# Fourier feature products of a diffusion backbone: from 4-byte operand pairs to 16-bit pairs with a power-of-two scale

## The chip, the cores and the metric

The kernel runs on one core of a Trainium2 chip. The metric is the device time of one execution in microseconds, taken as the median of several runs. The core's engines each work through a queue of their own in order: TensorE (PE, its weight loads PEld), VectorE (DVE), ScalarE (ACT), GpSimd (POOL), and SyncE (SP), which issues the transfers.

## The reference

Two layers work on 2048 latent tokens and 256 context tokens of width 1024. One input projection feeds three groups of heads: 2-D Fourier mixing, chunked spatial gating, and attention with 8 heads. Each result is gated, the three are joined, and one output projection with a gated residual ends the layer. The part that matters here is the Fourier group:

```python
def _fourier(u):
    b, n, _ = u.shape
    ug = u.astype(jnp.float32).reshape(b, n, F_GROUPS, F_GROUP_DIM).transpose(0, 2, 1, 3)
    f = jnp.fft.fft2(ug, norm="ortho").real
    return f.transpose(0, 2, 1, 3).reshape(b, n, F_WIDTH).astype(u.dtype)
...
    f_out = (_fourier(f_in) @ w_fmix) * jax.nn.silu(f_gate)
```

F_WIDTH is 256. The transform along the 64 features of a group is folded into the input projection and into `w_fmix`; the transform along the tokens is done in the kernel.

## The kernel before, in words

**Precision.** Nearly every product works on pairs: a value is split into a high and a low half, and `mm3` issues three matmuls into one accumulator, high x high, high x low, low x high. Almost everywhere the halves are 16-bit floats (F16). The last step of the Fourier group and the output projection still use 4-byte halves (F32R).

**The order.** The whole program is first recorded as a list of operations in program order (`Plan`). Then `schedule` lays them out by a list scheduler with a price for each operation (`cost`), planned ends of transfers, buffer counts and a look-ahead, and issues them; each engine's order is pinned to what came out. The three matmuls of an `mm3` are one operation (`plan.group`). The price of a matmul by the kind of its moving operand:

```python
        elif rhs.dtype == F16:
            d = n / 2.4 + 3.4 if args[1].shape[0] > 64 else n / 4.8 + 75.0
        else:
            d = max(190.0, n / 2.4 + 15.0)
```

with n the columns, and 20 more for a group of F16 matmuls.

**Stages.** In a layer, blocks of token tiles are normed and projected (`block`), with matmuls into `pj`. Then comes `attention`: for 8 heads, blocks of four query tiles run over 18 key tiles in pairs. A pair takes six matmuls for the scores (`sc`), two exponentials per key tile on ScalarE (`pp`, and `pw` or `sc` in place), one subtraction per key tile for the low half, on GpSimd for three of four and on VectorE for the fourth (`pp`), and, a few pairs later, 18 matmuls with the values (`pv`). Ahead of them run the maxima of the scores: matmuls into two banks of `mx`, and a VectorE reduction of each, with a small transposed shift at the end of a block (`mneg`, `mh`, `m`, `h`). After attention comes the output projection (`mixed`, `outward`).

**The background.** Work that attention does not need is fed in between the pairs by a generator, `background`: from the tenth pair on, two turns per pair. Its first part is `fourier`, where each `yield` stands for 6 turns in layer 0 and 8 in layer 1; then follow the modulation vectors of the gate and, in layer 0, the preparation of the next layer's weights, which includes several calls of `power`.

**`fourier`.** It loads the mixing weights of the layer (`wfm`, 128 x 4 x 256), adds and subtracts pairs of them (`first`) and splits the three results into `fm` with `split` (a ScalarE copy for the high half, a subtraction on GpSimd for the low one). It loads the 16 projected tiles into `X` and forms a butterfly over them on VectorE. For each of 9 frequency classes (and 2 of the context in layer 0) `finish` makes F16 halves `V`, multiplies them with trigonometric tables `ct`, splits the result `o` into `st0` and `st1`, and multiplies these with `fm`. Classes 1 to 7 are used twice: a mirrored copy `sr` of the halves serves the mirrored frequencies. That makes 18 such products in layer 0 and 16 in layer 1, each of two `mm3`. The result is multiplied with the column `back`, which undoes the scales, and with the gate `fg`, and is stored.

**`power`.** It turns a column of maxima into a scale: a transpose on TensorE, a VectorE maximum of one row, four one-element VectorE operations that give a power of two and its inverse, a TensorE product with a row of ones that spreads both over the partitions, and a VectorE copy.

Of the kernel before, what the change touches and what calls it, by code (L numbers as in the profile page):

```python
# [10 lines left out]
F32 = mybir.dt.float32  # L11
F32R = mybir.dt.float32r
F16 = mybir.dt.float16
# [8 lines left out]
P = 128  # L22
# [41 lines left out]

GK, GQ, G1, G2, G3 = 416, 512, 512, 256, 512
TOP = 14
PTOP, CTOP = 29, 14
KTOP = 11
EXPO = 0x7F800000

# [479 lines left out]
def hybrid_kernel(ctx: ExitStack, tc: tile.TileContext, a: dict, out: bass.AP):  # L550
# [3 lines left out]
    def mk(p, shape, dt, tag, bufs=None):  # L554
        return plan.tile(p, shape, dt, tag, bufs or p.bufs)
# [25 lines left out]
    def f(ap):  # L581
        return ap.bitcast(F32)
# [106 lines left out]
    def split(hi, lo, x, leng=None):  # L689
        act.activation(out=hi, in_=x, func=AF.Copy)  # L690
        (leng or dve).tensor_tensor(out=lo, in0=x, in1=f(hi), op=ALU.subtract)
# [578 lines left out]
    CA, CB = math.cos(math.pi / 8), math.sin(math.pi / 8)  # L1270

    def fourier(l, y, pf):
        back = mk(pf, [P, 1], F32, "back", 1)
        dve.tensor_scalar(out=back, in0=y["ic"][1], scalar1=2.0 ** (PTOP - CTOP), scalar2=None, op0=ALU.mult)
        fm = mk(pf, [P, 6, 256], F32R, "fm", 1)
        wfm = mk(pf, [P, 4, 256], F32, "wfm", 1)
        sp.dma_start(out=wfm, in_=a["w_fmix"][l].rearrange("k p n -> p k n"))
        first = wfm[:, 0]
        flip = column(C_FLIP)
        for s in range(3):  # L1280
            w, z = wfm[:, 2 * (s > 0)], wfm[:, 2 * (s > 0) + 1]
            if s == 2:
                dve.tensor_scalar(out=w, in0=w, scalar1=flip, scalar2=None, op0=ALU.mult)
            dve.tensor_tensor(out=first, in0=w, in1=z, op=ALU.subtract if s == 1 else ALU.add)
            split(fm[:, 2 * s], fm[:, 2 * s + 1], first, pool)
            yield

        def finish(re, im, cs, views):

            ct = mk(pf, [P, 4, P], F16, "ct")  # L1290
            sp.dma_start(out=ct, in_=cs)
            V = [mk(pf, [P, 2, 256], F16, f"V{q}") for q in range(2)]
            n = P + 4
            parts = [(0, re, slice(0, n), 1.0), (1, re, slice(n, 256), -1.0)]
            if im is not None:
                parts += [(0, im, slice(n, 256), 1.0), (1, im, slice(0, n), 1.0)]
            for v, x, s, sg in parts:
                act.activation(out=V[0][:, v, s], in_=x[:, s], func=AF.Copy, scale=sg)
                dve.scalar_tensor_tensor(out=V[1][:, v, s], in0=x[:, s], scalar=sg, in1=V[0][:, v, s], op0=ALU.mult, op1=ALU.subtract)
            if im is None:  # L1300
                for q in range(2):
                    dve.tensor_scalar(out=V[q][:, 0, n:], in0=re[:, n:], scalar1=0.0, scalar2=None, op0=ALU.mult)
                    dve.tensor_scalar(out=V[q][:, 1, P:n], in0=re[:, P:n], scalar1=0.0, scalar2=None, op0=ALU.mult)
            o = bank([P, 2, P])
            for g in range(2):
                gs_ = slice(g * P, (g + 1) * P)
                two = g == 1 or im is not None
                mm3(o[:, g], V[0][:, 0, gs_], V[1][:, 0, gs_], ct[:, 0], ct[:, 1], True, not two)
                if two:
                    mm3(o[:, g], V[0][:, 1, gs_], V[1][:, 1, gs_], ct[:, 2], ct[:, 3], False, True)  # L1310
            sh_ = [mk(pf, [P, 2, P], F32R, f"st{q}") for q in range(2)]
            split(sh_[0], sh_[1], o)
            for gate_rows, out_rows, w in views:
                if w == 4:
                    sr_ = [mk(pf, [P, 2, P], F32R, f"sr{q}", 1) for q in range(2)]
                    for s, r in zip(sh_, sr_):
                        dve.tensor_copy(out=r, in_=f(s)[:, :, ::-1])
                    sh_ = sr_
                fg = mk(pf, [P, 256], F32, "fg")
                sp.dma_start(out=fg, in_=gate_rows)  # L1320
                o = bank([P, 256])
                mm3(o, sh_[0][:, 0], sh_[1][:, 0], fm[:, 0], fm[:, 1], True, False)
                mm3(o, sh_[0][:, 1], sh_[1][:, 1], fm[:, w], fm[:, w + 1], False, True)
                dve.scalar_tensor_tensor(out=fg, in0=o, scalar=back, in1=fg, op0=ALU.mult, op1=ALU.mult)
                sp.dma_start(out=out_rows, in_=fg)

        X = mk(pf, [P, NCK, 256], F32, "X", 1)
        W = mk(pf, [P, 8, 256], F32, "W", 1)
        Q = mk(pf, [P, 8, 256], F32, "Q", 1)
        if l < DEPTH - 1:  # L1330
            for t in range(CT):
                sp.dma_start(out=Q[:, t], in_=p_d[t])
            pool.tensor_tensor(out=Q[:, 2], in0=Q[:, 0], in1=Q[:, 1], op=ALU.add)
            pool.tensor_tensor(out=Q[:, 3], in0=Q[:, 0], in1=Q[:, 1], op=ALU.subtract)
            gv, mv = (v.rearrange("(t k) f -> k t f", k=CT) for v in (fgc_d, mfc_d))
            for k in range(CT):
                finish(Q[:, 2 + k], None, a["cs_c"][k], [(gv[k], mv[k], 2)])
                yield
        for t in range(NCK):
            sp.dma_start(out=X[:, t], in_=p_d[CT + t])  # L1340

        def tt_(o, i0, i1, op):
            dve.tensor_tensor(out=o, in0=i0, in1=i1, op=op)

        def ts_(o, i0, k):
            dve.tensor_scalar(out=o, in0=i0, scalar1=k, scalar2=None, op0=ALU.mult)

        def lin(o, i0, k0, i1, k1):
            ts_(o, i0, k0)
            dve.scalar_tensor_tensor(out=o, in0=i1, scalar=k1, in1=o, op0=ALU.mult, op1=ALU.add)  # L1350

        A_, S_ = ALU.add, ALU.subtract
        x = lambda i, n=1: X[:, i:i + n]
        w = lambda i, n=1: W[:, i:i + n]
        q = lambda i, n=1: Q[:, i:i + n]
        gv, mv = (v.rearrange("(t k) f -> k t f", k=NCK) for v in (fgx_d, mfx_d))

        def both_ways(k):
            r = [(gv[k], mv[k], 2)]
            if 0 < k < NCK // 2:  # L1360
                r.append((gv[NCK - k], mv[NCK - k], 4))
            return r

        def fin(k, re, im):
            finish(re[:, 0], None if im is None else im[:, 0], a["cs_x"][k], both_ways(k))

        tt_(w(0, 8), x(0, 8), x(8, 8), A_)
        yield
        tt_(x(8, 8), x(0, 8), x(8, 8), S_)
        yield  # L1370
        tt_(x(0, 4), w(0, 4), w(4, 4), A_)
        yield
        tt_(x(4, 4), w(0, 4), w(4, 4), S_)
        yield
        tt_(w(0, 2), x(0, 2), x(2, 2), A_)
        yield
        tt_(w(2, 2), x(0, 2), x(2, 2), S_)
        yield
        tt_(x(0), w(0), w(1), A_)
        yield  # L1380
        tt_(x(1), w(0), w(1), S_)
        yield
        fin(0, x(0), None)
        yield
        fin(8, x(1), None)
        yield
        fin(4, w(2), w(3))
        yield
        tt_(w(6), x(5), x(7), S_)
        tt_(w(7), x(5), x(7), A_)  # L1390
        yield
        ts_(w(6, 2), w(6, 2), R2)
        tt_(x(2), x(4), w(6), A_)
        tt_(x(3), x(4), w(6), S_)
        yield
        tt_(w(4), x(6), w(7), A_)
        tt_(w(5), w(7), x(6), S_)
        fin(2, x(2), w(4))
        yield
        fin(6, x(3), w(5))  # L1400
        yield
        rev = X[:, 15:12:-1]
        tt_(q(0, 3), x(9, 3), rev, S_)
        yield
        tt_(q(3, 3), x(9, 3), rev, A_)
        ts_(x(4), q(1), R2)
        ts_(x(5), q(4), R2)
        yield
        tt_(x(6), x(8), x(4), A_)
        tt_(x(7), x(8), x(4), S_)  # L1410
        tt_(x(9), x(5), x(12), A_)
        yield
        tt_(x(10), x(5), x(12), S_)
        lin(x(11), q(0), CA, q(2), CB)
        lin(x(13), q(0), CB, q(2), -CA)
        yield
        lin(x(14), q(3), CB, q(5), CA)
        lin(x(15), q(3), CA, q(5), -CB)
        tt_(q(0), x(6), x(11), A_)
        yield  # L1420
        tt_(q(4), x(14), x(9), A_)
        fin(1, q(0), q(4))
        yield
        tt_(q(1), x(6), x(11), S_)
        yield
        tt_(q(5), x(14), x(9), S_)
        fin(7, q(1), q(5))
        yield
        tt_(q(2), x(7), x(13), A_)
        yield  # L1430
        tt_(q(6), x(15), x(10), A_)
        fin(3, q(2), q(6))
        yield
        tt_(q(3), x(7), x(13), S_)
        yield
        tt_(q(7), x(15), x(10), S_)
        fin(5, q(3), q(7))
        yield
# [440 lines left out]
```

## Time and profile before

| | |
|---|---|
| median of 3 runs | 3146.82 us (3145.03 to 3150.45) |
| profiled execution | 3142.39 us, of it a span of 3140.6 us |
| mean granted TensorE clock | 0.973 |
| attention with background, layer 0 | about 640 to 1440 us |
| attention with background, layer 1 | about 2195 to 2930 us |
| instructions | 64404 |

Nearly every operation is recorded at one line, L448, so the groups are told apart by engine, operation and the names of the tiles they write and read. TensorE's busy time is a model: matmuls are pipelined and their recorded ends overlap the next ones, so the starts tell more than the durations.

### The profile page before, as it was taken

The numbers are of one execution on the slowest core, as the hardware profiler recorded it, in microseconds if no ns is written. First come the engines' busy times: TensorE is split into PE (matmuls) and PEld (weight loads), VectorE is DVE, ScalarE is ACT, GpSimd is POOL, SyncE is SP. The second block draws the span as 40 slices with busy tenths as digits, with TensorE's granted clock in tenths as the row PEclk, the third lists the DMA queues.
The fourth block names the chain that finished last, engine by engine and source line by source line (L and its number), as shares of the span: only waits on it lengthen the run. The fifth ranks groups of instructions, "written<-read, shape, count | busy, mean of one in ns | idle before, by whom it ended". The sixth has DMA issues, their size and how long they took to land.

```text
span 3140.6 us, 64404 instructions
## 1 busy us (share of the span) xinstructions
PE 2953.2 (94%) x23194; PEld 1724.2 (55%) x23194; DVE 2458.5 (78%) x6740; ACT 1826.3 (58%) x3904; POOL 1693.5 (54%) x1836
## 2 busy tenths in 40 slices
PE   6789999899999999998999999998999999999899
PEld 3445555445554555556785454553555555555687
DVE  7878788789999978765638888887899989887332
ACT  4553444167777788883006644531887887888400
POOL 3564444357667777772004744542876777777300
PEclk8899999999999999999999999998999999999999
DMA  7333344422324322205535343345023241230342
GB/s 271 69 73 58 84 94 87 102 88 67 86 61 131 81 72 61 57 23 177 175 118 192 62 86 86 87 96 142 24 64 79 71 125 49 61 75 20 111 134 81
DMA packets 487865, 289.08 MB, mean 92 GB/s; under 512 B 372316, under 2 KB 424180, under 8 KB 487544
## 3 DMA queue, kind: packets, MB, share of 16 engines
q1 hardware_dynamic: 487544, 284.96, 35.1%
q8 instruction: 182, 2.98, 0.4%
q14 instruction: 139, 1.14, 0.1%
HBM read 193.18 MB, written 91.66 MB: 91 GB/s over the span
## 4 chain that ended last, share of the span: by engine, by line
PE 59%; DVE 20%; DMA 8%; ACT 6%; POOL 3%; issue 2%; SPq 2%; DVEq 0%; ACTq 0%; POOLq 0%
PE pj L448 20%; PE sc L448 16%; PE pv L448 10%; PE mx L448 9%; DVE k L448 6%; DVE mx L448 4%; PE cb L448 3%; DMA k<-d 2%; ACT k L448 2%; SPq L448 2%; POOL k L448 2%; ACT pp L448 1%; DVE ns_t L448 1%; DMA mw<-in_w_modT_dram 1%; ACT pw L448 1%
## 5 line engine op out<-in xcount | busy, mean ns | idle before, releaser
L448 POOL TENSOR_TENSOR pp<-pw,pp 128x512 f16<-128x512 f32 (+1 forms) x876 | 1021.0, 1183 | 395.9 <-ACT pw L448 317.6
L448 PEld LDWEIGHTS <-h 128*128 128x128 f16 (+2 forms) x7008 | 581.8, 98 | 772.2 <-issue 410.2
L448 DVE TENSOR_REDUCE mx<-mx 128x1 f32<-128x512 f32 (+1 forms) x1296 | 770.9, 626 | 142.9 <-PE mx L448 136.9
L448 ACT ACTIVATE pp<-sc 128x512 f16<-128x512 f32 (+1 forms) x1168 | 717.5, 615 | 228.8 <-PE sc L448 215.5
L448 PE MATMUL sc<-h,h 128*128 128x512 f16 (+1 forms) x2336 | 602.8, 380 | 4.1 <-ACT pw L448 1.7
L448 ACT ACTIVATE pw<-sc 128x512 f32<-128x512 f32 (+1 forms) x876 | 543.7, 621 | 0.6 <-POOL pp L448 0.6
L448 PEld LDWEIGHTS <-pp 128*128 128x128 f16 x10432 | 467.3, 98 | 115.1 <-issue 32.5
L448 PE MATMUL pv<-k,pp 128*128 128x65 f16 (+2 forms) x10432 | 507.6, 203 | 7.6 <-DVE sm L448 7.0
L448 PE MATMUL mx<-h,h 96*128 96x512 f16 (+1 forms) x1296 | 410.4, 366 | 34.9 <-DVE mx L448 25.5
L448 PE MATMUL pj<-wh,h 128*128 128x512 f32 x1088 | 361.9, 405 | 7.3 <-DVE k L448 7.1
L448 PEld LDWEIGHTS <-hp 128*128 128x128 f16 x1920 | 187.8, 99 | 176.0 <-issue 14.3
L448 PE MATMUL pj<-w,h 128*128 128x512 f16 (+1 forms) x1296 | 272.2, 349 | 4.8 <-DVE tm L448 3.6
L448 PE MATMUL pj<-w,hp 128*128 128x512 f16 (+1 forms) x1152 | 241.4, 347 | 8.5 <-DVE tm L448 4.5
L448 POOL TENSOR_TENSOR h<-k,h 128x512 f16<-128x512 f32 (+1 forms) x72 | 80.8, 1138 | 299.6 <-ACT h L448 298.4
L448 PEld LDWEIGHTS pj<-wh,h 128*128 128x128 f32 x1088 | 208.6, 192 | 56.7 <-DVE k L448 11.1
L448 DVE TENSOR_TENSOR pp<-sc,pp 128x512 f16<-128x512 f32 (+1 forms) x292 | 197.8, 677 | 42.6 <-ACT sc L448 39.7
L448 PE MATMUL sc<-h 40*128 40x512 f16 (+1 forms) x1168 | 228.2, 387 | 0.0
L448 PE MATMUL pj<-wl,h 128*128 128x512 f32 x544 | 216.8, 399 | 0.0
L448 PE MATMUL pj<-h,h 128*128 128x416 f16 (+2 forms) x912 | 201.7, 363 | 6.5 <-ACT h L448 5.0
L448 DVE TENSOR_TENSOR pj<-pj,gr 128x512 f32<-128x512 f32 x68 | 47.3, 698 | 187.3 <-PE pj L448 187.3
L448 PE MATMUL pj<-h,hp 128*128 128x512 f16 (+1 forms) x768 | 174.4, 365 | 6.4 <-ACT hp L448 3.3
L448 ACT ACTIVATE sc<-sc 128x512 f32<-128x512 f32 (+1 forms) x292 | 178.8, 612 | 0.0
(270 smaller groups left out, 3936.7 us busy)
## 6 DMA issues: line engine op xcount, KB each, us to landing
d<-k SPq DMA_DIRECT2D x560, 48.0 KB
d<-k SPq DMA_DIRECT2D x166, 128.0 KB
d<-k SPq DMA_DIRECT2D x70, 256.0 KB
k<-d SPq DMA_DIRECT2D x132, 128.0 KB
k<-d SPq DMA_DIRECT2D x66, 256.0 KB
h<-d SPq DMA_DIRECT2D x24, 432.0 KB
d<-vt SPq DMA_DIRECT2D x144, 65.0 KB
k<-d SPq DMA_DIRECT2D x16, 585.0 KB
```

The lines of the kernel that those rows point to most:

```text
L448: r = getattr(getattr(self.nc, eng), method)(*args, **kw)
```

## The change

The Fourier products along the features get 16-bit halves. The mixing weights of a layer are first multiplied by one power of two that brings their greatest magnitude to a fixed size: a maximum over `wfm`, `power`, and a scaling on ScalarE. The results that meet them are multiplied by the fixed factor 2^-16 as they are split. `back` takes in the inverse of both. `fm`, `st` and `sr` become F16. After the scaling there is one more `yield`.

```diff
-PTOP, CTOP = 29, 14
+PTOP, CTOP, STOP, FTOP = 29, 14, 16, 13
...
     def fourier(l, y, pf):
-        back = mk(pf, [P, 1], F32, "back", 1)
-        dve.tensor_scalar(out=back, in0=y["ic"][1], scalar1=2.0 ** (PTOP - CTOP), scalar2=None, op0=ALU.mult)
-        fm = mk(pf, [P, 6, 256], F32R, "fm", 1)
+        fm = mk(pf, [P, 6, 256], F16, "fm", 1)
         wfm = mk(pf, [P, 4, 256], F32, "wfm", 1)
         sp.dma_start(out=wfm, in_=a["w_fmix"][l].rearrange("k p n -> p k n"))
+        am = mk(small, [P, 1], F32, "fa", 1)
+        dve.tensor_reduce(out=am, in_=wfm.rearrange("p k n -> p (k n)"), axis=AX.X, op=ALU.max, apply_absolute_value=True)
+        fw = mk(pf, [P, 2], F32, "fw", 1)
+        power(am, fw, FTOP)
+        back = mk(pf, [P, 1], F32, "back", 1)
+        dve.tensor_scalar(out=back, in0=fw[:, 1:], scalar1=y["ic"][1], scalar2=2.0 ** (PTOP - CTOP + STOP), op0=ALU.mult, op1=ALU.mult)
+        act.activation(out=wfm, in_=wfm, func=AF.Copy, scale=fw[:, 0:1])
+        yield
...
             dve.tensor_tensor(out=first, in0=w, in1=z, op=ALU.subtract if s == 1 else ALU.add)
-            split(fm[:, 2 * s], fm[:, 2 * s + 1], first, pool)
+            act.activation(out=fm[:, 2 * s], in_=first, func=AF.Copy)
+            pool.tensor_tensor(out=fm[:, 2 * s + 1], in0=first, in1=fm[:, 2 * s], op=ALU.subtract)
             yield
...
-            sh_ = [mk(pf, [P, 2, P], F32R, f"st{q}") for q in range(2)]
-            split(sh_[0], sh_[1], o)
+            sh_ = [mk(pf, [P, 2, P], F16, f"st{q}") for q in range(2)]
+            act.activation(out=sh_[0], in_=o, func=AF.Copy, scale=2.0 ** -STOP)
+            dve.scalar_tensor_tensor(out=sh_[1], in0=o, scalar=2.0 ** -STOP, in1=sh_[0], op0=ALU.mult, op1=ALU.subtract)
...
-                    sr_ = [mk(pf, [P, 2, P], F32R, f"sr{q}", 1) for q in range(2)]
+                    sr_ = [mk(pf, [P, 2, P], F16, f"sr{q}", 1) for q in range(2)]
                     for s, r in zip(sh_, sr_):
-                        dve.tensor_copy(out=r, in_=f(s)[:, :, ::-1])
+                        dve.tensor_copy(out=r, in_=s[:, :, ::-1])
```

## The prediction

> **What bounds the kernel now.** I began with the page's busy shares, then cut the span into the stretches where the Fourier work runs, then read the chain of waits in those stretches, and last the instructions that the change touches. In the stretches the columns are length, busy time (and instructions) of PE, PEld, DVE, ACT and POOL, then the granted clock, the DMA share and GB/s.
>
> ```profile
> PE 2953.2 (94%) x23194; PEld 1724.2 (55%) x23194; DVE 2458.5 (78%) x6740; ACT 1826.3 (58%) x3904; POOL 1693.5 (54%) x1836
> 705.00:930.00 225.00, 220.03 (x2298) 127.13 (x2297) 218.43 (x488) 173.85 (x382) 153.10 (x141) 1.00 0.28 72
> 2210.00:2545.00 335.00, 332.28 (x3550) 189.75 (x3548) 311.37 (x636) 275.89 (x580) 244.95 (x221) 1.00 0.23 59
> ```
> ```profile
> by line: DVE mx L448 21.3%; PE sc L448 21.2%; PE pv L448 11.1%; PE mx L448 9.7%; DVE pp L448 5.3%; PE cb L448 3.8%; issue 3.6%; DVE X L448 3.0%; DVE Q L448 2.3%; DVE mneg L448 2.3%; DVE V L448 2.3%; DVE h L448 2.2%; DVE sr L448 1.6%; DVE fg
> by line: PE sc L448 38.3%; PE pv L448 23.9%; PE mx L448 17.0%; PE cb L448 5.6%; DVE mx L448 3.7%; DMA h<-d 2.4%; ACT pp L448 1.2%; DVE V L448 1.2%; ACT pw L448 1.2%; DVE pp L448 0.9%; issue 0.9%; DVE m L448 0.7%; DVE fg L448 0.4%; DVE mh L4
> ```
> The Fourier work has no stage of its own: it is strewn into attention, in layer 0 mostly at 705 to 930 us and in layer 1 at 2210 to 2545 us. In layer 1 TensorE bounds: its lines sc, pv, mx and cb make 84.8% of the chain. In layer 0 TensorE (220 of 225 us) and VectorE (218 of 225) are both full, and TensorE holds only 45.8% of the chain. So a us saved on TensorE is worth about 0.85 us in layer 1 and 0.46 us in layer 0, and VectorE work is nearly free in neither.
>
> **The products themselves.** The change turns 204 matmuls, 68 groups of three, from 4-byte to 16-bit operands.
>
> ```profile
> L448 PEld LDWEIGHTS cb<-fm,st x120: 186/189/203, 723.1 to 2536.9; 128*128 128x128 f32 x120
> L448 PE MATMUL cb<-fm,sr x84: 274/282/473, 812.6 to 2538.9; 128*128 128x256 f32 x84
> L448 PEld LDWEIGHTS <-V 128*128 128x128 f16 x222 | 16.2, 97 | 11.2 <-issue 6.9 <-DVE V L448 0.7
> ```
> The weight loads would halve, from 189 to 97 ns. But a load runs beside the matmul ahead of it, so what counts is the time that a group holds TensorE. The chain, in order of time, gives this (start, us, what):
>
> ```profile
> 722.50 0.81 PE pv L448 x18
> 723.31 0.41 PE cb L448 x3
> ...
> 2402.61 0.32 PE mx L448
> 2402.93 0.36 PE cb L448 x3
> 2403.29 0.23 PE mx L448
> ...
> 2404.60 1.19 PE sc L448 x6
> 2405.79 0.55 PE cb L448 x3
> ```
> ```profile
> 526.54 2.62 PE pj L448 x24
> ```
> The last row is 24 matmuls of the wanted form (16-bit, 256 columns): 0.109 us each, 0.33 us for three. A group of today takes 0.36 behind mx, 0.41 behind pv, and 0.55 behind sc; there about 0.10 belongs to leaving the 40-row matmuls and stays (mx behind sc takes 0.32 instead of 0.22 to 0.23), so the comparable figure is 0.45. Going through TensorE's order, 36 of the 68 groups stand behind mx, 12 behind pv, 20 behind sc (the rows are one of each kind). Savings: 36 x 0.03 + 12 x 0.08 + 20 x 0.12 = 1.1 + 1.0 + 2.4 = 4.4 us of TensorE. 36 groups are in layer 0 and 32 in layer 1: 2.3 x 0.46 + 2.1 x 0.85 = 1.1 + 1.8 = 2.9 us of the end. Bounds: 0.03 x 68 = 2 us, and 0.22 x 68 = 15 us if every group cost 0.55 and fell to 0.33.
>
> The Trainium skill ("TensorE: Matmul & The Clock Gate", section on weight-path perf modes) says that fast weight load is on for 128 weights of a type other than FP32; our two load rows agree in size (189 against 97 ns). Taken as time of TensorE, its rule would give 204 x 92 ns = 18.8 us, an estimate by that page; the same page (section on the architectural detail of the array) lets loads be pulled ahead of running matmuls, and the 0.36 us row is with that second rule: the sum goes by the row.
>
> **The copies and splits.** Same counts on the same engines, other types.
>
> ```profile
> L448 DVE CAST sr<-st x28: 277/287/1254, 809.2 to 2534.9; 128x256 fp32r<-128x256 f32 x28
> L448 DVE TENSOR_TENSOR st<-cb,st x20: 406/414/426, 722.6 to 2534.4; 128x256 fp32r<-128x256 f32 x20
> L448 DVE SCALAR_TENSOR_TENSOR vt<-mx,vt 128x512 f16<-128x512 f32 x36 | 24.4, 679 | 1.1 <-ACT vt L448 1.1
> L448 POOL TENSOR_TENSOR fm<-wfm,fm x6: 723/727/775, 658.0 to 2214.7; 128x256 fp32r<-128x256 f32 x6
> L448 DVE TENSOR_TENSOR k<-mx,f 128x512 f32<-128x512 f32 x36 | 24.6, 682 | 0.2
> ```
> The low half of the results becomes one fused multiply-subtract from PSUM: at 512 columns that form takes 679 ns and the plain one 682, so nothing changes. ScalarE's high half gets a constant factor: nothing. GpSimd's low half of the weights writes 2 bytes instead of 4: six instructions, nothing. The 28 reversed copies take 287 ns. With the 131 ns of a one-element instruction (row below) as the fixed part, half the column time would leave 0.21 us (28 x 0.08 = 2.2 us of VectorE gained), while a reversed 16-bit read at full column time would take the 414 ns of the st row (28 x 0.13 = 3.6 us lost). With VectorE's share of the path a bit over a half in layer 0 and small in layer 1 that is -0.6 to +1.2 us; I take 0, the cell in the middle. The Trainium skill ("VectorE: DVE Perf Modes", what auto-detection checks) puts a 16-bit copy in SBUF with step 1 or -1 at four per cycle and a 4-byte one at two; by it the lower end would hold, 0.6 us, and no row here shows such a copy.
>
> **The new power of two.** Per layer it adds: a maximum over 128x1024 and six small instructions on VectorE, a transpose and two tiny matmuls on TensorE, a 128x1024 scaling on ScalarE that the three adds and splits wait for, and one more pause of the generator. No DMA is added.
>
> ```profile
> L448 DVE TENSOR_REDUCE am<-w x48: 396/664/686, 49.7 to 1705.8; 128x1 f32<-128x512 f32 x32, 128x1 f32<-128x256 f32 x16
> L448 DVE TENSOR_SCALAR pe<-pe x56: 130/131/142, 39.3 to 1748.0; 1x1 int32<-1x1 int32 x42, 1x1 f32<-1x1 f32 x14
> L448 DVE TENSOR_REDUCE pe<-cb x14: 268/272/279, 38.9 to 1746.0; 1x1 f32<-1x128 f32 x14
> L448 ACT ACTIVATE k<-k 128x1024 bf16<-128x1024 f32 x36 | 38.1, 1058 | 46.3 <-DMA k<-in_x_dram 17.2 <-DMA k<-d 15.8 <-DMA k<-in_ctx_dram 5.4
> 1123.86 0.11 PE cb L448
> 1127.81 0.31 PE cb L448 x2
> 1128.16 0.16 DVE L448 COPY cg<-cb 128x2 f32<-128x2 f32 x1 [0.81 <-PE cb L448]
> ```
> VectorE: the maximum is 0.67 + 2 x 0.27 = 1.2 us (256 columns more cost 0.27); the small ones 0.27 + 4 x 0.13 + 0.16 = 0.95. TensorE: 0.11 + 0.31 = 0.42 us. ScalarE: 1.06 us. `back` only changes its operands.
>
> Where does this land? Instructions are placed where the planner thinks the weights have arrived. In layer 0 they arrive late, and everything stops behind VectorE (start, us, engine; the idle time before in brackets):
>
> ```profile
> 650.11 0.43 DVE L448 TENSOR_TENSOR wfm<-wfm 128x256 f32<-128x256 f32 x1 [3.99 <-DMA wfm<-in_w_fmix_dram]
> 651.19 1.19 PE L448 MATMUL mx<-h,h 96*128 96x512 f16 x2 [3.67 <-DVE mx L448]
> 654.66 0.60 ACT L448 ACTIVATE pp<-sc 128x512 f16<-128x512 f32 x1 [4.17 <-PE sc L448]
> 2190.22 2.99 DVE L448 TENSOR_REDUCE mx<-mx 128x1 f32<-128x512 f32 x5 [0.15 <-PE mx L448]
> 2190.97 1.18 PE L448 MATMUL mx<-h,h 96*128 96x512 f16 x2 [0.35 <-DVE mx L448]
> ```
> The maximum takes the first add's place behind that transfer: the stop of 4 us stays, and the maxima of the scores queued behind it, for which TensorE waits, come 1.2 us later; the small instructions count by VectorE's share, 0.4. Layer 0: +1.6. In layer 1 the same work falls into the end of the prologue, where VectorE runs maxima nearly without a gap and TensorE waits for them: again +1.2 + 0.4 = +1.6. TensorE's 2 x 0.42 at a mean share of 0.65: +0.5. ScalarE's 2 x 1.06: 0, covered by its idle time (174 of 225 and 276 of 335 us busy); uncovered, +2.1. The products themselves do not wait: the last weights are split by 2215 us in layer 1, long ahead of the first use there, and in layer 0 the first use is at 723.1. The extra pause moves the rest of the background work by 3 pairs of key tiles in layer 0 and 4 in layer 1. By the code the background takes two turns per pair, and in layer 0 it needs 32 x 6 + 16 x 4 + 18 x 4 = 328 turns of some 570, so it ends well before the attention, and I put the shift at nothing; its cover are these some 240 turns.
>
> **Sum.** -2.9 + 1.6 + 1.6 + 0.5 = +0.8 us. Against the profiled execution (3142.39 us, span 3140.6) that is 3143.2; that execution stands 4.4 us under the median of 3146.82, so the forecast for the median is 3147 us to the nearest us. The bounds of the parts give -15 to -2 for the products, -0.6 to +1.2 for the copies, +2 to +6 for the power. About 0.2%, 6.3 us, is what a measurement of this kernel can tell from no change; the forecast is no change.
>
> **Rivals.** (1) Loads are exposed after all, and a tighter order helps. The planner prices a 4-byte product at 190 ns and a 16-bit one at 110, so the order of every engine is drawn up anew with 15 us less of TensorE. If all 68 groups gave 0.22 us on the path, 15 - 3.7 = 11 us are gained: 3136. For it: the 0.55 rows and the 189 ns loads. Against: the 0.36 rows, and VectorE's 218 of 225 us in layer 0. (2) The other side: ScalarE is caught by the scaling. It stands in ScalarE's queue ahead of exponentials and waits for a chain VectorE, TensorE, VectorE, TensorE, VectorE. The same chain for other weights did this:
>
> ```profile
> 2202.15 0.87 PE L448 MATMUL pv<-k,pp 128*128 128x65 f16 x18
> 1056.50 1.49 PE L448 MATMUL pv<-k,pp 128*128 128x65 f16 x18
> 1056.80 0.61 ACT L448 ACTIVATE wf<-uq,cu 128x384 f32<-128x384 f32 x1 [4.62 <-DVE cu L448]
> ```
> ScalarE stood 4.6 us, and afterwards TensorE ran at half its pace (pv 1.49 us where 0.87 is usual), together about 6 us; the next such chain, of the 1123.86 to 1128.16 rows above, cost under 1 us. One such stop makes 3153 to 3154, two 3160. It decides as soon as VectorE is more than some 4 us behind its planned place when the chain starts, and in layer 0 it starts right behind a transfer that was 4 us late. Against: that lateness stopped TensorE and ScalarE as well, so they are equally late. (3) The new order shifts other stops. Waits for transfers, such as these, sit where the order puts them:
>
> ```profile
> 1249.10 8.14 DMA h<-d
> 1257.30 7.89 DMA wf<-in_w_out_dram
> ```
> One such stop of 8 us more or less: 3139 or 3155.
>
> **Chances.** Forecast 0.43; rival 1 0.18; rival 2 0.20; rival 3 0.19, of it 0.10 faster. So faster 0.28, within 0.2% 0.43, slower 0.29. The likeliest case's own range is 3141 to 3153; with the rivals 3134 to 3161, from all of rival 1 to two stops of rival 2.
>
> **What the profile of the changed kernel would show.** The loads of fm's products at 97 ns; three of them 0.33 us behind mx or pv in the chain, 0.43 behind sc; a maximum over wfm of 1.2 us behind the same wait of 4 us; ScalarE's scaling without a wait of more than 1 us ahead of it; reversed copies at 0.21 or at 0.41 us. Wrong would be: a wait of several us on fw, a group of more than 0.45 us, or a difference that sits outside 640 to 940 and 2180 to 2560 us, which would be the new order and not the change itself.

## The result, and the profile after

The changed kernel takes 3124.64 us (median of 4 runs, 3122.28 to 3127.4) beside 3145.93 us (4 runs, 3139.53 to 3150.45) for the kernel before: a ratio of 0.9934, 95% interval 0.9914 to 0.9954. The forecast was no change, 3147 us, with 3134 as the lower end; the time lies 9 us below that end. The profiled execution took 3122.28 us with a span of 3120.5 (before: 3142.39 and 3140.6).

The first line is from the page, busy time by engine; the next three are the stretches of the prediction, moved to where the same work now runs, and the one at 1000 to 1070 us, which the prediction did not look at (length, busy time and instructions of PE, PEld, DVE, ACT, POOL, granted clock, DMA share, GB/s).

```profile
PE 2937.9 (94%) x23200; PEld 1710.9 (55%) x23200; DVE 2445.2 (78%) x6754; ACT 1829.3 (59%) x3906; POOL 1687.6 (54%) x1836
705.00:930.00 225.00, 220.47 (x2355) 125.65 (x2355) 219.30 (x492) 180.20 (x393) 157.43 (x147) 1.00 0.25 71
1000.00:1070.00 70.00, 66.00 (x666) 34.63 (x666) 68.71 (x177) 59.16 (x124) 55.62 (x52) 1.00 0.31 82
2200.00:2535.00 335.00, 332.86 (x3580) 187.26 (x3578) 305.07 (x648) 279.67 (x588) 247.83 (x225) 1.00 0.22 59
```

The same stretch of the kernel before:

```profile
1000.00:1070.00 70.00, 62.53 (x568) 31.78 (x568) 64.68 (x163) 49.54 (x106) 46.21 (x43) 0.90 0.31 76
```

In the stretch with most of layer 0's Fourier work, TensorE gets through 57 more matmuls in the same 225 us (2355 for 2298). But in the 70 us after 1000, where no product of the change is left, it gets through 98 more (666 for 568), and the granted clock is 1.00 for 0.90. From the first to the last score matmul, layer 0 takes 778.1 us for 787.9 (-9.8) and layer 1 725.1 for 734.3 (-9.2); all else together is 1.1 us less. So the gain lies in both layers' attention, and not only where the changed instructions run.

The same columns over the two attentions, first of the kernel before, then of the changed one; the last two rows are stretches of the kernel before:

```profile
639.00:1426.90 787.90, 762.04 (x7892) 425.08 (x7891) 666.66 (x1496) 635.52 (x1336) 570.81 (x534) 0.98 0.27 70
2194.40:2928.70 734.30, 722.86 (x7654) 398.86 (x7653) 632.50 (x1307) 615.68 (x1268) 552.08 (x497) 0.99 0.24 62
636.80:1414.90 778.10, 752.46 (x7895) 418.46 (x7894) 662.96 (x1503) 637.11 (x1337) 566.65 (x534) 0.99 0.26 71
2184.00:2909.10 725.10, 716.83 (x7657) 394.48 (x7656) 624.33 (x1314) 616.15 (x1269) 549.65 (x497) 1.00 0.23 62
1009.00:1015.80 6.80, 6.21 (x17) 1.65 (x17) 4.07 (x12) 2.13 (x5) 3.87 (x4) 0.50 0.17 39
1053.30:1060.10 6.80, 5.80 (x45) 3.70 (x44) 6.08 (x18) 1.14 (x2) 0.91 (x1) 0.50 0.82 195
```

TensorE stands idle just as long in layer 0 as before (25.9 us, then 25.6); in layer 1 the idle time falls from 11.4 to 8.3 us. What changed most in layer 0 is the clock. The granted clock of these traces is either 1.00 or 0.50. In layer 0's attention it is at 0.50 for 27.3 us in the kernel before and for 13.7 in the changed one: the two spells of 6.8 us in the last two rows are gone. In layer 1 it is 9.2 and 4.1 us. If TensorE loses half of such time, that makes 6.8 of the 9.8 us in layer 0 and 2.6 of the 9.2 in layer 1; this is an estimate.

The instructions of the change, by tile (count, min/median/max ns, first and last start):

```profile
L448 PE MATMUL cb<-fm,st x120: 270/272/283, 718.2 to 2526.7; 128*128 128x256 f16 x120
L448 PEld LDWEIGHTS <-sr x84: 95/98/100, 816.7 to 2529.6; 128*128 128x128 f16 x84
L448 DVE COPY sr<-st x28: 208/214/1137, 812.2 to 2525.9; 128x256 f16<-128x256 f16 x28
L448 POOL TENSOR_TENSOR fm<-wfm,fm x6: 666/672/720, 695.4 to 2243.6; 128x256 f16<-128x256 f32 x6
L448 DVE TENSOR_REDUCE fa<-wfm x2: 1220/1220/1220, 648.1 to 2185.0; 128x1 f32<-128x1024 f32 x2
L448 DVE COPY fw<-cb x2: 158/158/159, 691.8 to 2216.2; 128x2 f32<-128x2 f32 x2
L448 ACT ACTIVATE wfm<-wfm,fw x2: 1132/1144/1157, 692.1 to 2216.9; 128x1024 f32<-128x1024 f32 x2
```

The chain of waits in layer 1, in order of time:

```profile
2386.61 1.19 PE sc L448 x6
2387.80 0.43 PE cb L448 x3
2388.23 0.22 PE mx L448
2388.45 0.33 PE cb L448 x3
...
2405.79 0.71 PE pv L448 x18
2406.50 0.33 PE cb L448 x3
```

A group of three now takes 0.33 us behind mx and pv and 0.43 behind sc, the three numbers of the forecast. And the timeline at the stops that the prediction named (start, us, engine, instruction; in brackets the idle time before and what ended it):

```profile
648.07 1.22 DVE L448 TENSOR_REDUCE fa<-wfm 128x1 f32<-128x1024 f32 x1 [4.15 <-DMA wfm<-in_w_fmix_dram]
649.94 0.58 PE L448 MATMUL mx<-h,h 96*128 96x512 f16 x1 [4.62 <-DVE mx L448]
1055.83 0.63 ACT L448 ACTIVATE wf<-uq,cu 128x384 f32<-128x384 f32 x1
2184.98 1.22 DVE L448 TENSOR_REDUCE fa<-wfm 128x1 f32<-128x1024 f32 x1
2755.02 0.63 ACT L448 ACTIVATE wh<-wf 128x512 fp32r<-128x512 f32 x1 [3.04 <-DMA wf<-in_w_out_dram]
```

```profile
2770.26 0.63 ACT L448 ACTIVATE wh<-wf 128x512 fp32r<-128x512 f32 x1 [5.07 <-DMA wf<-in_w_out_dram]
2772.27 0.27 PE L448 MATMUL mx<-h,h 96*128 96x256 f16 x1 [3.18 <-DVE mx L448]
```

The second fence is the kernel before. Two stops that have nothing to do with the Fourier group changed: ScalarE's wait of 4.62 us for the scale `cu` (1056.80 us in the prediction) is gone, and the wait of 5.07 us for output weights, behind which TensorE stood for 3.18 us, fell to 3.04 and no longer stops TensorE.

### The profile page after: what moved, and what is told of

It is laid out like the page before. It is cut to its first block, busy times and chain, and to the rows that moved or that the text cites. A ratio compares the mean times of both kernels' runs of the same rounds, so it can differ in the third digit from the quotient of the medians.

```text
span 3120.5 us, 64453 instructions
## 1 busy us (share of the span) xinstructions
PE 2937.9 (94%) x23200; PEld 1710.9 (55%) x23200; DVE 2445.2 (78%) x6754; ACT 1829.3 (59%) x3906; POOL 1687.6 (54%) x1836
## 3 DMA queue, kind: packets, MB, share of 16 engines
q14 instruction: 139, 1.14, 0.1%
## 4 chain that ended last, share of the span: by engine, by line
PE 62%; DVE 17%; DMA 8%; ACT 6%; POOL 3%; issue 2%; SPq 2%; DVEq 0%; ACTq 0%; POOLq 0%
PE pj L448 19%; PE sc L448 18%; PE pv L448 11%; PE mx L448 10%; DVE k L448 6%; PE cb L448 3%; DVE mx L448 3%; ACT k L448 2%; SPq L448 2%; DMA k<-d 2%; POOL k L448 2%; DMA k<-in_x_dram 1%; DVE ns_t L448 1%; DMA mw<-in_w_modT_dram 1%; ACT pp L448 1%
```

## The experiments

Two theories were set against each other. **Width**: the products' own time is what pays. **Order**: the planner lays out every engine anew after any edit, and where the stops fall then decides. (Width is P in the first expectations and W in the later ones, order is O.) Later a third was added, M, that products and an order priced for them pay only together. `plan.price = (p, g)` in the diffs replaces the planner's price of one product matmul by p ns and of its group by g more; it changes no instruction, only the order. Ratios are to the kernel before, which stood at 3148.6 to 3149.5 us in these comparisons; the changed kernel's own 0.9934 is from the first one, where it stood at 3145.93. A ratio on record and the quotient of the two medians differ by up to 0.1%.

### Price and content apart

**e1_old_price**: the changed kernel, its products priced as before.

```diff
+                plan.price = (190.0, 0.0)
                 mm3(o, sh_[0][:, 0], sh_[1][:, 0], fm[:, 0], fm[:, 1], True, False)
                 mm3(o, sh_[0][:, 1], sh_[1][:, 1], fm[:, w], fm[:, w + 1], False, True)
+                plan.price = None
```

> The changed kernel, with its 16-bit products priced in the planner as the 4-byte ones were (190 ns a matmul, nothing added for the group); all instructions are those of the changed kernel, only their order is another. Theory P (the products themselves give it all): the ratio to the kernel before stays at 0.993 to 0.994. Theory O (products give 5 to 7 us, the rest is stops that the new order moved): the group of three products still takes 0.33 us and the gain over the kernel before is at least 5 us, but the rest changes: a ratio anywhere from 0.991 to 0.999, with a difference to the changed kernel that sits in a few stops of TensorE of 3 us and more outside the Fourier stretches.

Measured: 3139.46 us, 0.9970 (0.9959 to 0.9982). Less than half of the gain.

**e2_new_price**: the kernel before, its 4-byte products priced as 16-bit ones: the same two lines with `(256 / 2.4 + 3.4, 20.0)`.

> The kernel before, with its 4-byte products priced in the planner as the 16-bit ones are (110 ns a matmul, 20 for the group); no instruction is another, only the order. Theory P: ratio 0.999 to 1.001. Theory O: the order alone moves stops of 5 to 8 us each; a ratio from 0.995 to 1.004, with the difference in a few stops. If the tighter price by itself were what helps: 0.996 or less.

Measured: 3148.78 us, 1.0001 (0.9991 to 1.001). A cheaper price by itself brought nothing in this order.

**e3_power_only**: the kernel before with the maximum, `power`, the scaling and the pause; the halves stay 4 bytes wide.

```diff
+        am = mk(small, [P, 1], F32, "fa", 1)
+        dve.tensor_reduce(out=am, in_=wfm..., op=ALU.max, apply_absolute_value=True)
+        fw = mk(pf, [P, 2], F32, "fw", 1)
+        power(am, fw, FTOP)
...
+        act.activation(out=wfm, in_=wfm, func=AF.Copy, scale=fw[:, 0:1])
+        yield
```

> The kernel before with the maximum, the power of two, the scaling and the extra pause, but 4-byte halves: the change without its products. Theory P: the added work costs its 2 to 4 us, ratio 1.0005 to 1.0015. Theory O: this is the part that shifts the background by a pause, so the stops at the weights' power of two in layer 0 (near 1052 us) and at the output weights in layer 1 (near 2765 us) change here too: ratio 0.994 to 0.998, and the added work shows no wait of more than 1 us.

Measured: 3141.71 us, 0.9979 (0.997 to 0.9988). Work was added and the kernel became faster.

**e4_products_only**: the changed kernel without those lines; the mixing weights are split unscaled.

> The changed kernel without the maximum, the power of two, the scaling and the extra pause; the mixing weights are split unscaled, so the low halves keep fewer bits. The change's products alone. Theory P: ratio 0.993 or a little under. Theory O: products and copies give 5 to 7 us, ratio near 0.998, with stops of 5 to 8 us more or less on either side of it: 0.995 to 1.000, and the stop near 1052 us stays since the background keeps its place.

Measured: 3129.04 us, 0.9930 (0.9917 to 0.9942). The whole gain, without the power of two. This is in theory P's range and below theory O's, and the stop near 1052 us, which O expected to stay, is down to 0.40 us. Together the four contradict a plain sum of parts: -0.70% for the products here, -0.30% for products and power in e1, -0.21% for the power in e3.

### The same order, the other width

To take the order out, each of four orders was run with both widths: every changed instruction is priced as the one that it replaces (products, and the six low halves on GpSimd), and `back` is made where the kernel whose order is taken makes it. So the planner draws the same lists: in the traces of each pair every engine has the same instructions in the same order. A pair differs in operand types, in the forms of mirrored copies and low halves, and in constant factors, so a row measures products, copies and splits together.

```diff
+                plan.price = (190.0, 0.0)             # e7, e9; e8, e10: (256 / 2.4 + 3.4, 20.0)
+        ...; d = d if not (two and o.t.tag == "fm") else 150 + n * 2.1    # e7, e9; e8, e10: 1.87
```

> 16-bit products without the power of two, in exactly the order of the kernel before (each changed instruction is priced for the planner as the 4-byte one was, so every engine's list is the same but for the operand types). The kernel before stands at 3146 us. Theory W (the products' own time is what pays): the groups give back 0.11 to 0.17 us each by the excess over the plain matmul times around them, 7.5 to 11.5 us of TensorE for 68, of which 5 to 9 us reach the end: 3137 to 3141. Theory O (the order alone pays, by where it puts stops): the old order keeps its stops, 3143 to 3147. Theory M (products and an order priced for them pay only together): 3140 to 3147.

> The kernel before with 4-byte products, in exactly the order of the kernel with the 16-bit products alone (3129 us). Theory W: slower than that kernel by the products' own 5 to 9 us: 3134 to 3138. Theory O: the good order pays whatever the width: 3129 to 3132. Theory M: an order priced too low for what is in it gives back everything: 3144 to 3150.

> The whole change (power of two, pause, 16-bit products) in exactly the order of the kernel with the power of two and 4-byte products (3141.7 us). W: 3133 to 3137. O: 3139 to 3142. M: 3137 to 3142, since the order is priced for the 4-byte products.

> 4-byte products with the power of two and the pause, in exactly the order of the changed kernel (3124.6 us). W: 5 to 9 us slower than the changed kernel, 3130 to 3134. O: 3125 to 3128. M: 3140 to 3148.

| order of | 4-byte products | 16-bit products | difference |
|---|---|---|---|
| the kernel before | 1 | e7: 0.9980 (0.997 to 0.999), 3141.79 us | -0.20% |
| e4 (products only) | e8: 0.9943 (0.9929 to 0.9957), 3129.95 us | e4: 0.9930 | -0.13% |
| e3 (power only) | 0.9979 | e9: 0.9966 (0.9953 to 0.9978), 3136.78 us | -0.13% |
| the changed kernel | e10: 0.9948 (0.9934 to 0.9963), 3132.57 us | 0.9934 | -0.14% |

Down a column the order changes, along a row the width. The width gives 0.13 to 0.20% in each of the four, on average 0.15% or 4.7 us, with an interval of about 0.09% to either side; by itself only the first difference is clear of its interval. (The last row joins two comparisons; by medians in us it would be 7.9 us, 0.25%.) The order gives up to 0.57% (18 us) at the old width. The average width is just under the 5 to 9 us of theory W, and the larger part is theory O's. Single runs do not tell W from O: e9 and e10 lie in W's range, e8 in O's, and e7 between the two, 0.8 us above W's and 1.2 below O's. The third theory falls: e8 and e10, 4-byte products in orders priced for 16-bit ones, keep four fifths of the gain.

The stops go with the order. Timeline and stretch of e7, 16-bit products in the old order:

```profile
1057.27 0.61 ACT L448 ACTIVATE wf<-uq,cu 128x384 f32<-128x384 f32 x1 [4.63 <-DVE cu L448]
2770.49 0.63 ACT L448 ACTIVATE wh<-wf 128x512 fp32r<-128x512 f32 x1 [4.86 <-DMA wf<-in_w_out_dram]
1000.00:1070.00 70.00, 63.69 (x608) 33.43 (x606) 65.48 (x165) 51.05 (x108) 48.49 (x44) 0.93 0.30 77
```

and of e10, 4-byte products in the order of the changed kernel:

```profile
1061.32 0.63 ACT L448 ACTIVATE wf<-uq,cu 128x384 f32<-128x384 f32 x1
2767.59 0.63 ACT L448 ACTIVATE wh<-wf 128x512 fp32r<-128x512 f32 x1 [2.17 <-DMA wf<-in_w_out_dram]
1000.00:1070.00 70.00, 64.83 (x636) 33.16 (x634) 68.85 (x181) 55.76 (x118) 50.96 (x49) 0.98 0.33 87
```

e7 has both stops of the kernel before, to within 0.3 us, and the clock is at 0.50 in two spells of this stretch (3.4 us from 1013.5 and 6.8 from 1054.4 us). e10, with the old operands, lacks the first stop and has less than half of the second, and one spell of 3.4 us is left (from 1002.4 us). In e8, whose TensorE stands idle least of all in layer 0's attention (18.2 us of 771.8), the stretch shows 684 matmuls:

```profile
1000.00:1070.00 70.00, 67.64 (x684) 36.28 (x683) 67.06 (x176) 60.72 (x127) 57.39 (x55) 1.00 0.34 81
```

What ends TensorE's waits between 700 and 1240 us, by the view of waits (total us, times, longest), first in the kernel before, then in e8, then in the changed kernel:

```profile
PE mx L448 <- DVE mx L448: 11.2, 19, 1.7
```

```profile
PE mx L448 <- DVE mx L448: 3.0, 7, 1.0
```

```profile
PE mx L448 <- DVE mx L448: 9.2, 18, 3.0
```

The same instructions in the first two: VectorE's maxima are late for TensorE 19 times in one order and 7 times in the other. The changed kernel has nearly as many late maxima here as the kernel before; its gain in layer 0 goes with the two missing spells at half clock, and only in layer 1's attention do its late maxima cost clearly less (9 times, 3.7 us in all, for 12 times and 6.4). What sets off a spell stays open: in the kernel before, waits of 1.02 and 0.41 us stand just ahead of the one at 1053.3 us, while a wait of 3.05 us in the changed kernel, which ended at 964.6 us, was followed by none.

### Is it the price, or is each order a draw?

e2 and e8 have the same instructions and differ in two small things, the planner's price of six GpSimd instructions (688 or 629 ns) and the place of `back` in program order, and lie 18 us apart. From the end of layer 0's background work on, every engine's order is the same in both. TensorE gets there at 1133.3 us in e2 and at 1117.0 in e8, and the attention of layer 1 then takes 734.0 us in both. Four more orders of the kernel before, all with its own instructions:

```diff
+        yield                                  # e5: ahead of "first = wfm[:, 0]"
+                plan.price = (210.0, 0.0)      # e18
+                plan.price = (120.0, 20.0)     # e15, with the six low halves at 1.87
+                plan.price = (100.0, 20.0)     # e16, likewise
```

> The kernel before with nothing but the extra pause of the background generator ahead of the mixing weights: the same instructions in a new order. The kernel before stands at about 3147 us in these comparisons; the power of two with its pause, 4-byte products kept, at 0.9979 of it. Theory R (each redrawn order is a draw of its own, whatever the reason it was redrawn): anywhere from 3129 to 3149. Theory S (an order improves when the products are priced near 110 ns, and otherwise stays): 3143 to 3149. Theory D (the added instructions cost their 3 us, and the pause makes up for more): 3136 to 3141.

> The kernel before with the planner's price of a Fourier feature product set to 210 ns instead of 190: the same instructions in a new order, priced further from 110. R: 3129 to 3149. S: not faster than before, 3144 to 3152.

> The kernel before with that price at 120 ns and the group's 20, and the six low halves on GpSimd priced as 16-bit ones: the same instructions in a new order, close in price to the one that stood at 0.9943 and to the one that stood at 1.0001. R: 3129 to 3149. S: 3126 to 3137.

> The same with a price of 100 ns: the same instructions in a new order. R: 3129 to 3149. S: 3126 to 3137.

Measured: e5 3137.56 us, 0.9963 (0.9951 to 0.9976); e18 3141.67, 0.9977 (0.9969 to 0.9986); e15 3151.16, 1.001 (0.9999 to 1.0021); e16 3139.59, 0.9968 (0.9957 to 0.9978). The price has no direction: 120 ns is the slowest of all, 100 and 210 are alike. So theory S falls. Theory R fits, though its range is wide and e15 lies 2 us above it. The pause alone gives 0.37%. It is not a pure redraw: in e5 the pause stands ahead of the first use of the weights, the add comes at 657.94 us without a wait, and TensorE's stop of 3.67 us near 651 is gone; in e3 and the changed kernel the maximum, ahead of the pause, keeps the wait for the transfer (3.74 and 4.15 us). (Theory D allows for e5 too: with e3 at 0.9979 the added instructions would then cost 0.16%, 5 us. But the orders of e3 and e5 differ as well, by a scatter larger than that, so D is neither shown nor excluded.)

Nine orders with 4-byte products now stand (1, e2, e3, e5, e8, e10, e15, e16, e18; two of them with the power of two, and e2 and e8 alike in their later part): mean 0.9977, standard deviation 0.24% (7.5 us), 0.9943 to 1.001. The order of the kernel before is among the three slowest. e15 shows the same sign at 1000 us as the kernel before, clock 0.90:

```profile
1000.00:1070.00 70.00, 63.02 (x590) 32.09 (x588) 65.07 (x173) 46.62 (x98) 40.98 (x39) 0.90 0.28 71
```

### Are the layers separate draws, and the changed kernel's order one of them?

```diff
+        if l == 1:                    # e19; e20: l == 0
             am = ...
             ...
             yield
+        else:
+            dve.tensor_scalar(out=back, in0=y["ic"][1], scalar1=2.0 ** (PTOP - CTOP + STOP), ...)
```

In the layer left out, the weights are split unscaled. e21 is the changed kernel with `plan.price = (120.0, 20.0)`, e6 the changed kernel without the `yield` behind the scaling.

> The changed kernel with the power of two, the scaling and the pause in layer 1 alone; layer 0 has the 16-bit products with unscaled weights. By the lists of instructions, layer 0 runs in the order of the kernel with the products alone (whose attention there ended 18.9 us earlier than before's), layer 1 in the order of the changed kernel (9.2 us earlier). Theory L (each layer's order is its own draw and the gains add): 28 us under before less nothing in between, 0.991 of it, 3118 to 3122. Theory T (what a layer gains depends on the other, by transfers or the clock): 3124 to 3130.

> The converse: power of two in layer 0 alone, so layer 0 in the order of the changed kernel (9.8 us earlier than before's) and layer 1 in that of the products alone (5.0 us). L: 15 us under before, 0.9952, 3130 to 3135. T: 3122 to 3129.

> The changed kernel, its products priced at 120 ns instead of 110 for the planner: the same instructions in another order. Theory R (its order is one draw among others, which so far lie at 0.9943 to 1.001 with a mean of 0.9977, and the width gives 0.14% in any of them): anywhere in 0.993 to 0.9995, most likely 0.996 (3135). Theory S (the change's own price and structure make its order good): 0.9925 to 0.9945, 3123 to 3130.

> The changed kernel without the extra pause: the same instructions in another order, the background work some pairs earlier. R: 0.993 to 0.9995, most likely 0.996 (3135). S, where the pause is what makes the order good: 0.998 or more (3141); where it does nothing: 0.9925 to 0.9945.

| | ratio | us | attention, layer 0 | layer 1 |
|---|---|---|---|---|
| before | 1 | 3148.59 | 787.9 | 734.3 |
| e4 | 0.9930 | 3129.04 | 769.2 | 729.3 |
| changed kernel | 0.9934 | 3124.64 | 778.1 | 725.1 |
| e19: layer 0 of e4, layer 1 of the change | 0.9883 (0.9868 to 0.9898) | 3114.57 | 771.3 | 725.7 |
| e20: the converse | 0.9945 (0.9933 to 0.9958) | 3131.94 | 781.7 | 728.5 |
| e21 | 0.9913 (0.9899 to 0.9926) | 3120.94 | 772.3 | 723.5 |
| e6 | 0.9957 (0.9945 to 0.997) | 3134.08 | 781.0 | 728.7 |

(Attention in us from the start of the first to that of the last score matmul in the profiled executions; e4 and the changed kernel were timed in other comparisons than the last four.) A layer's order brings its time along, to within 4 us, whatever the other layer does: theory L, though the median of e19 came out 3 us below its range. e19 beats both kernels; it does without the power of two in layer 0. e6 lies in theory R's range and outside S's; e21 came out faster than both allow (0.9913 for 0.993 and 0.9925 at the least), so R's spread was put too narrow and S does not hold either. The changed kernel redrawn (e21, e6, and e1 and e9 above) lies at 0.9913 to 0.997, on average with itself 0.9948: its 0.9934 is one draw and not the best. This average is 0.29% under that of the nine orders above; the width is 0.15% of it, and the rest is within the scatter.

## Why the prediction was wrong

**Products.** The forecast of 4.4 us of TensorE was right, and for its reason. In the kernel before and e7, which share one order, the median time from the start of the matmul ahead of a group to the start of the one behind it fell from 588 to 548 ns behind mx (36 groups), 467 to 383 behind pv (12) and 778 to 657 behind sc (20): 36 x 0.040 + 12 x 0.084 + 20 x 0.121 = 4.9 us. The share that reaches the end was put at 2.9 us; the mean of the four rows is 4.7 us, with the copies in it, which is nearly TensorE's saving in full. In the profiled executions of the four pairs the attention of layer 0 became shorter by 2.5 us on average and that of layer 1 by 2.3, so the weight of 0.46 for layer 0 has no support; but single pairs scatter from 0.3 to 4.7 us, and the difference isn't shown. The rule of the Trainium skill ("TensorE: Matmul & The Clock Gate", weight-path perf modes), taken as time of TensorE, would have been 18.8 us, an estimate by that page; the chain after (0.33 and 0.43 us) goes with 4.9. Loads halved as forecast, 189 to 98 ns.

**Copies.** 214 ns for 287: the lower end, 28 x 0.073 = 2.0 us of VectorE, where the middle was taken. The Trainium skill ("VectorE: DVE Perf Modes", what auto-detection checks) lets a 16-bit copy in SBUF with step -1 run in its fourfold mode. By it the lower end, 0.21 us by estimate, was to hold; the trace agrees. The fused low half took 410 ns for 414, no change as forecast.

**Power of two.** The pieces had their sizes: maximum 1.22 us (forecast 1.2), copy 0.16, scaling 1.14 (1.06). In layer 0 the stop at the weights' transfer stayed and TensorE's wait behind it grew from 3.67 to 4.62 us, 0.95 for the 1.2 forecast. In layer 1 the first 24 pairs took 59.1 us, before 59.7: none of the 1.6 us forecast is seen. So of the 3.7 us some 1 us can be pointed to. What the power of two costs in a fixed order was not measured, since its instructions were only run in new orders; the 3.7 us are neither shown nor refuted.

**Rivals.** ScalarE was not caught (rival 2): no instruction waited for `fw` in either layer. Its example was misread as well: the slow pv at 1056.50 us did not come after ScalarE's stop, which ended at 1056.80; it lies in the spell at half clock that began at 1053.3 us. Rival 1 gave 3136 by 0.22 us a group, where 0.04 to 0.12 were measured, and by a tighter order, which a lower price did not bring (e2, e15). Rival 3, other stops, is nearest to what happened: it had a chance of 0.10 on the faster side and a size of one stop, 8 us, where the order of the changed kernel gave 0.52% (e10, with the power of two), 16 us. It looked for waits on transfers; what these runs show to have changed is more than that, the spells at half clock above all.

**The step that failed** is the one that put the new order at nothing: "The extra pause moves the rest of the background work ... I put the shift at nothing; its cover are these some 240 turns." The cover was there (the background ends near 1125 us, the attention at 1415) and was beside the point. The pause alone gave 0.37%, 12 us (e5). Every engine's list is redrawn over both attentions, and a redraw moves this kernel by 7.5 us (one standard deviation of the nine orders), more than twice the largest term of the sum. The start was also taken as a neutral order; it is among the slowest seen, so that by the mean of the nine a redraw was to be expected 0.23% faster. That this redraw gave more than twice that is luck as far as the runs show: the same instructions in four other orders (e21, e6, e9, e1) came out anywhere from 0.9913 to 0.997. The sign given for being wrong, a difference outside 640 to 940 and 2180 to 2560 us, did show: 1000 to 1070 us, and 2770. With the term as measured the sum is -16 (order, with the power of two in it) - 4 (width) = -20 us. This is no check of the account, since the two rows of e10 and the changed kernel make up that difference between them. (The sum of the prediction, +0.8 us on 3146.82, is 3147.6, which rounds to 3148 and not 3147; nothing hangs on it.)

## What to carry to other kernels

Where a planner orders the queues, any edit, a pause or a price included, is two changes: its own cost and a redraw of the order. Price the first on a fixed order (let the planner charge the new instructions the old price), and measure the scatter of the second with a few orders of unchanged code before crediting a gain to the edit. Layers that are planned one after the other are separate draws: joining the layer-0 order of one kernel to the layer-1 order of another gave far more here (0.9883) than the edit's own 0.15%.

## What the runs showed of the hardware that was not expected

A VectorE copy of 128x256 with reversed columns takes 214 ns at 16 bits and 287 ns at 4 bytes: no row has the same copy without the reversal, so what the reversal itself costs isn't shown. GpSimd's subtraction of 128x256 became faster with a 16-bit second operand and output, 672 for 727 ns. The 4-byte operands show inside a group too: behind sc, the first and last of its three matmuls start 341 ns apart, with 16-bit operands 229 ns; whether the loads (189 and 98 ns) or the moving operand make the difference these runs don't separate. And the granted clock falls to 0.50 for 3.4 or 6.8 us at a time within layer 0's attention, in places that shift with the order; it can do so near waits of 1 us and not do so after one of 3.05 us.
